# Weights' tiles moved to another offset in their buffers: 64 and 128 bytes between what TensorE moves and what it loads next

## The chip, the cores and the metric

The kernel runs on 1 core of a Trainium2 chip. The metric is the device time of one execution in microseconds (us). Before the change the median of 3 runs is 1715.13 us (1715.05 to 1716.48).

## The reference

One layer of an encoder block runs on two groups of tokens, 256 (prompt) and 512 (sample), with the same weights, all in float32. D_MODEL is 1024. What matters here are the first dense products of the layer:

```
h    = rmsnorm(x, norm_mix_g)
proj = h @ w_in                       # 1024 x 8192
u, q, k, v, qm, gl = split(proj)      # S5 input, differential attention's q, k, v,
                                      # memory attention's queries, gate logits
kv   = rmsnorm(mem, mem_norm_g) @ w_mem_kv   # keys and values of 256 memory tokens a group
```

u goes through a state-space model (S5), q, k, v through attention with two softmax maps a head, qm with kv through cross-attention. The three results are projected (w_branch), gated with sigmoid(gl + b_gate), summed and projected (w_out); then comes a gated feed-forward network (w_gate_up, w_down). Results are added to x.

## The kernel before

**Products in three parts.** A float32 operand is split into a high part (rounded to float32r) and a low part (the rest). `mm3` (L845 to L848) makes one product of two split operands from three matmuls: high x high (L846), high x low (L847) and low x high (L848). In a matmul, TensorE holds one operand still (the stationary one, 128 x 128, which a weight load, LDWEIGHTS, brings in ahead) and streams the other (the moved one, here mostly 256 columns). While one matmul streams, the next one's stationary operand is loaded.

**Which operand is which.** `dense_fm` (L850) gives feature-major results: the weights are stationary, the activations move. It makes gl (L1263, 12 pairs of weights' tiles, 256 columns a matmul), the memory queries mq (L1021) and u (L1225, 256 and 512 columns). `dense_tm` (L870) gives token-major results: the activations are stationary, the weights move. It makes qk (L1329), v (L1361), and the memory keys mk (L980) and values mv (L1001), all with 256 moved columns. The activations are H (the normed x, made by `whole_pair`, L938) and MT (the normed memory, called memThi and memTlo). A sum over 1024 features takes 8 steps of `mm3`, so 24 matmuls make one output tile; this document calls them a unit.

**The weights' stream.** `WStream` (L541) holds an ordered list of weights' pieces (`W.add`, L780 to L815), each with a kind. `_dma` (L572) loads half a piece with a DMA on SP's queue; `_split` (L667) splits it into a tile wh and a tile wl: ACT copies the high part (L679), and the low part is either subtracted by VectorE (L685) or, while `by_dma` is set (from gl on, L1256), copied negated by ACT (L682) and completed by a DMA on POOL's queue that adds (L683). `get` (L697) hands out the piece that is next and has the piece after it split. `_tile` (L586) allocates a pair of tiles in the pools whi and wlo, 4 buffers each. A tile has 1024 + 64 columns, of which 1024 are used; the used ones begin at column 0, or at column 32 where `shift` is set, which is the case for pieces of kind "s": the queries of memory and the gate logits. The tiles are 1088 x 4 = 4352 bytes apart, a multiple of 256. The very first piece (the first head's keys of memory) is not split by `_split` but piecemeal in the preamble (L1133 to L1142).

H's tiles are 6144 + 64 and 6144 + 16 columns, of which the first 16 are skipped (`c0=16`, L938). The order of the products is: keys, values and queries of memory, mixed with the attention over memory (to about 285 us); u; gl with the state-space model's products between (285 to 583 us); qk and v with the attention's products between (585 to 855 us); then the branches and the feed-forward network, whose products have 384 or 512 moved columns apart from the first block's.

```
c0, room = (32 if shift else 0), (0 if extra else 64)
t = [p.tile([128, self.HALF + room], F32R, name=f"w{w}{i}", tag=f"w{w}")
     for p, w in zip(self.extra if extra else (self.ph, self.pl), "hl")]
return tuple(x[:, c0 : c0 + self.HALF] for x in t)
```

Of the kernel before, what the change touches and what calls it, by code (L numbers as in the profile page):

```python
# [540 lines left out]
class WStream:  # L541
# [42 lines left out]
        self.n_dma += 1  # L584

    def _tile(self, i, extra=False, shift=False):  # L586
        c0, room = (32 if shift else 0), (0 if extra else 64)
        t = [p.tile([128, self.HALF + room], F32R, name=f"w{w}{i}", tag=f"w{w}")
             for p, w in zip(self.extra if extra else (self.ph, self.pl), "hl")]
        return tuple(x[:, c0 : c0 + self.HALF] for x in t)  # L590
# [120 lines left out]
def hybrid_block(ctx, tc, A, outs, consts):  # L711
# [17 lines left out]
    W = WStream(nc, tc, ctx)  # L729
# [38 lines left out]
    def cols(name, c0, n=256):  # L768
        w = A[name]
        return w.rearrange("(k p) c -> p k c", p=128)[:, :, c0 : c0 + n]  # L770
# [8 lines left out]
                 ("v", 3), ("q", 3)]  # L779
    for what, h in MEM_ORDER:  # L780
        c0 = {"k": 0, "v": 1024, "q": 4096}[what] + 256 * h
        W.add(cols("w_in" if what == "q" else "w_mem_kv", c0), 8, 256, "s" if what == "q" else None)
    for c in range(4):
        W.add(cols("w_u", 256 * c), 8, 256)
    for c in range(12):
        W.add(cols("w_in", 5120 + 256 * c), 8, 256, "s")
    for h in DIFF_HEADS:
        if h is None:
            W.add(cols("w_in", 3072 + 256 * vp), 8, 256)
        else:  # L790
            W.add([cols("w_in", 1024 + 128 * h, 128), cols("w_in", 2048 + 128 * h, 128)], 8, 256)
            vp = h // 2
    for nme in ("w_branch2", "s5_w_glu", "w_branch0", "w_branch1"):
        for c in range(4):
# [309 lines left out]
    with tc.tile_pool(name="nrm", bufs=1) as pool, tc.tile_pool(name="nrmg", bufs=1) as pg:  # L1104
# [19 lines left out]
        for k in range(8):  # L1124
            q, n = nc.sync if k else nc.scalar, 1 if k < 4 else 2
# [4 lines left out]
                pin(nc.scalar.dma_start(cg, A["gcols"]))  # L1130
        W.n_dma = W.n_split = 2
        W._dma()
        wp = [W._tile(f"0_{h}") for h in range(2)]  # L1133
        W.parts[0] = wp
        pss = [psd("mk"), env.psa("mk"), psd("mk"), env.psa("mk")]
        for k in range(8):
# [1085 lines left out]
```

## Time and profile before

| | |
|---|---|
| median of 3 runs | 1715.13 us |
| the profiled execution | 1715.91 us |
| its span, first to last instruction | 1714.1 us |
| granted TensorE clock, mean | 1.000 |
| TensorE (PE), matmuls | 1700.2 us busy, 99% of the span, 12082 matmuls |
| TensorE's weight loads (PEld) | 1624.3 us, 95% |
| VectorE (DVE) | 1313.2 us, 77% |
| ScalarE (ACT) | 931.8 us, 54% |
| GpSimd (POOL) | 337.1 us, 20% |

In the profile, a group's row has the source line, the engine, the operation, the tiles written and read, the shape, the count, then the busy time in us, the mean duration in ns, and the idle time before. A row of the timeline has the start in us, the duration in us, and the instruction. Matmuls are pipelined: a new one starts while the one before is still shown as running, and the ends are modelled. So the time that a matmul takes from the stream is the step from its start to the next one's start; durations serve to compare matmuls of one shape.

### The profile page before, as it was taken

The page shows a single profiled execution, that of the slowest core. Times are in us where ns is not written, and L with a number is a line of the kernel's source. Part 1 is how long each engine was busy: PE and PEld are TensorE (multiplying, and loading weights), DVE is VectorE, ACT ScalarE, POOL GpSimd, SP SyncE. Part 2 cuts the span into 40 slices and gives each one's busy share as a digit, 9 for nine tenths or more (in the row PEclk, how much of TensorE's full clock was granted, in tenths as well). Part 3 has the DMA queues.
Part 4 walks back from the last instruction along what each step waited for, and adds up shares of the span by engine and source line. Part 5 has one row for each costly group of instructions (what it writes and reads, how often), then busy time and mean ns, then how long its engine had stood idle before and what let it go on. Part 6 is the DMA issues. An engine that isn't in the chain of part 4 may idle for free.

```text
span 1714.1 us, 31468 instructions
## 1 busy us (share of the span) xinstructions
PE 1700.2 (99%) x12082; PEld 1624.3 (95%) x12082; DVE 1313.2 (77%) x2383; ACT 931.8 (54%) x1957; POOL 337.1 (20%) x403
## 2 busy tenths in 40 slices
PE   9999999999999999999999999999999999999999
PEld 9999988999999999999989999998889898989897
DVE  6876556999997459889876687792698868687876
ACT  6554536766665357778766564552444545454541
POOL 0040510000000111001210111430114334343420
PEclk9999999999999999999999999999999999999999
DMA  8433456676656446565964445672314448484733
GB/s 298 166 97 102 136 170 151 153 187 176 170 152 165 129 108 144 132 154 135 209 134 131 162 148 171 153 214 72 87 49 115 137 113 192 114 192 115 173 119 108
DMA packets 206758, 250.02 MB, mean 146 GB/s; under 512 B 34272, under 2 KB 162800, under 8 KB 206608
## 3 DMA queue, kind: packets, MB, share of 16 engines
q1 hardware_dynamic: 162896, 155.70, 30.0%
q0 software_dynamic: 32480, 67.01, 20.5%
q10 hardware_dynamic: 11232, 25.31, 4.3%
q8 instruction: 95, 1.56, 0.4%
q14 instruction: 55, 0.45, 0.1%
HBM read 173.51 MB, written 52.17 MB: 132 GB/s over the span
## 4 chain that ended last, share of the span: by engine, by line
PE 81%; issue 10%; DMA 4%; DVE 3%; ACT 1%; POOL 0%; SPq 0%; POOLq 0%; ACTq 0%; DVEq 0%
PE br L846 4%; PE br L847 4%; PE br L848 4%; PE up L846 3%; PE up L847 3%; PE up L848 3%; PE gate L847 3%; PE gate L848 3%; PE gate L846 3%; PE dn L846 3%; PE dn L848 3%; PE dn L847 3%; PE qk L847 3%; PE qk L846 3%; PE qk L848 3%
## 5 line engine op out<-in xcount | busy, mean ns | idle before, releaser
L846 PE MATMUL gl<-Hhi,wh 128*128 128x256 f32 x576 | 164.7, 286 | 0.5 <-ACT glt L1264 0.3
L847 PE MATMUL gl<-Hlo,wh 128*128 128x256 f32 x576 | 160.4, 278 | 0.0
L848 PE MATMUL gl<-Hhi,wl 128*128 128x256 f32 x576 | 160.2, 278 | 0.0
L679 ACT ACTIVATE wh<-wr 128x1024 fp32r<-128x1024 f32 x116 | 122.3, 1056 | 51.7 <-PE u L847 10.8
L683 POOL DMA_DIRECT2D wl<-wr x46 | 40.2, 874 | 463.5 <-ACT wl L682 440.3
L685 DVE TENSOR_TENSOR wl<-wr,wh 128x1024 fp32r<-128x1024 f32 x70 | 85.8, 1227 | 38.7 <-ACT wh L679 37.1
L846 PEld LDWEIGHTS gl<-Hhi,wh 128*128 128x128 f32 x576 | 108.4, 188 | 3.4 <-issue 1.8
L848 PEld LDWEIGHTS gl<-Hhi,wl 128*128 128x128 f32 x576 | 108.8, 189 | 0.0
L847 PEld LDWEIGHTS gl<-Hlo,wh 128*128 128x128 f32 x576 | 108.4, 188 | 0.2 <-issue 0.2
L846 PE MATMUL qk<-wh,Hhi 128*128 128x256 f32 x384 | 107.6, 280 | 0.0
L847 PE MATMUL qk<-wl,Hhi 128*128 128x256 f32 x384 | 107.5, 280 | 0.0
L848 PE MATMUL qk<-wh,Hlo 128*128 128x256 f32 x384 | 107.2, 279 | 0.0
L602 ACT ACTIVATE wh_S<-ws 128x512 fp32r<-128x512 f32 x91 | 53.9, 625 | 67.0 <-PE up L847 27.8
L607 DVE TENSOR_TENSOR wl_S<-ws,wh_S 128x512 fp32r<-128x512 f32 x91 | 67.0, 757 | 28.9 <-ACT wh_S L602 28.8
L846 PEld LDWEIGHTS qk<-wh,Hhi 128*128 128x128 f32 x384 | 72.3, 188 | 0.8
L848 PEld LDWEIGHTS qk<-wh,Hlo 128*128 128x128 f32 x384 | 72.3, 188 | 0.5
L847 PEld LDWEIGHTS qk<-wl,Hhi 128*128 128x128 f32 x384 | 72.2, 188 | 0.5
L1436 ACT ACTIVATE p<-sc,nm 128x512 f32<-128x512 f32 (+1 forms) x96 | 59.0, 617 | 13.2 <-DVE nm L1434 12.8
L1434 DVE TENSOR_REDUCE nm<-sc 128x1 f32<-128x512 f32 (+1 forms) x96 | 56.7, 599 | 11.5 <-PE sc L1428 10.5
L628 POOL TENSOR_TENSOR ws<-wr,ws 128x512 f32<-128x512 f32 x26 | 38.8, 1492 | 126.1 <-DVE wl_S L607 106.8
L602 ACT ACTIVATE wh_A<-wr 128x512 fp32r<-128x512 f32 x65 | 38.1, 623 | 39.0 <-PE up L847 17.3
L1264 ACT ACTIVATE glt<-gl,bg 128x256 f32<-128x256 f32 x72 | 33.6, 466 | 46.4 <-PE gl L848 34.8
(704 smaller groups left out, 6324.9 us busy)
## 6 DMA issues: line engine op xcount, KB each, us to landing
wl<-wr POOLq DMA_DIRECT2D x46, 512.0 KB, 5.6
wr<-in_w_gate_up_dram SPq DMA_DIRECT2D x44, 512.0 KB, 4.1
wr<-in_w_in_dram SPq DMA_DIRECT2D x40, 512.0 KB, 4.8
wr<-in_w_branch_dram SPq DMA_DIRECT2D x24, 512.0 KB, 3.9
wr<-in_w_down_dram SPq DMA_DIRECT2D x22, 512.0 KB, 4.4
gl_scr<-glt SPq DMA_DIRECT2D x72, 128.0 KB, 3.6
wr<-in_w_in_dram SPq DMA_DIRECT2D x32, 256.0 KB, 4.4
wr<-in_w_mem_kv_dram SPq DMA_DIRECT2D x14, 512.0 KB, 5.1
```

What stands on the lines that cost most here:

```text
L602: self.nc.scalar.activation(f(hi), src, AF.Copy)
L607: self.nc.vector.tensor_tensor(out=f(lo), in0=src, in1=f(hi).bitcast(F32), op=ALU.subtract)
L628: gt(out=s4, in0=A12, in1=s2, op=sub)
L679: self.nc.scalar.activation(hi, r, AF.Copy)
L683: self.nc.gpsimd.dma_start(lo, r.bitcast(F32R), accum_op=ALU.add)
L685: self.sub.tensor_tensor(out=lo, in0=r, in1=hi.bitcast(F32), op=ALU.subtract)
L846: pe.matmul(ps, wh, xh, start=start, stop=False)
L847: pe.matmul(ps, wh, xl, start=False, stop=False)
L848: pe.matmul(ps, wl, xh, start=False, stop=stop)
L1264: act.activation(gt[:, 0:n], ps[:, 0:n], AF.Identity, bias=bg[:, M : M + 1])
L1434: v.tensor_reduce(out=nm[:, m : m + 1], in_=ps, axis=AX.X, op=ALU.max, negate=True)
L1436: act.activation(pm[:, 0:n], ps, AF.Exp, bias=nm[:, m : m + 1], accum_out=s1s[:, tt : tt + 1] if m == 0 else s2)
```

## The change

The used columns of a tile of kind "s" begin at column 48 in place of 32. The keys and values of memory and the products of q with k and of v become kind "s" too, and the preamble's first pair of tiles is shifted in the same way. u, the branches and the feed-forward network are not touched. Sizes, the number of instructions and their order in the source stay.

```
     def _tile(self, i, extra=False, shift=False):
-        c0, room = (32 if shift else 0), (0 if extra else 64)
+        c0, room = (48 if shift else 0), (0 if extra else 64)
...
-        W.add(cols("w_in" if what == "q" else "w_mem_kv", c0), 8, 256, "s" if what == "q" else None)
+        W.add(cols("w_in" if what == "q" else "w_mem_kv", c0), 8, 256, "s")
...
     for h in DIFF_HEADS:
         if h is None:
-            W.add(cols("w_in", 3072 + 256 * vp), 8, 256)
+            W.add(cols("w_in", 3072 + 256 * vp), 8, 256, "s")
         else:
-            W.add([cols("w_in", 1024 + 128 * h, 128), cols("w_in", 2048 + 128 * h, 128)], 8, 256)
+            W.add([cols("w_in", 1024 + 128 * h, 128), cols("w_in", 2048 + 128 * h, 128)], 8, 256, "s")
...
-        wp = [W._tile(f"0_{h}") for h in range(2)]
+        wp = [W._tile(f"0_{h}", shift=True) for h in range(2)]
```

## The prediction

> **What bounds the kernel now.** I read the page first, then the groups by line with shapes kept apart, then the timeline of TensorE alone in narrow windows, because only starts are measured there: ends of matmuls are modelled.
>
> ```profile
> span 1714.1 us, 31468 instructions
> ...
> PE 1700.2 (99%) x12082; PEld 1624.3 (95%) x12082; DVE 1313.2 (77%) x2383; ACT 931.8 (54%) x1957; POOL 337.1 (20%) x403
> ...
> PE 81%; issue 10%; DMA 4%; DVE 3%; ACT 1%; POOL 0%; SPq 0%; POOLq 0%; ACTq 0%; DVEq 0%
> ```
>
> TensorE is busy 99% of the span and is 81% of the chain that ended last. So a nanosecond more or less between two matmuls moves the end by a nanosecond, wherever it stands. The profiled execution took 1715.91 us, 1.8 us more than its span, and 0.78 us more than the median of 1715.13.
>
> These are the matmuls that the change touches, all with 256 moved columns:
>
> ```profile
> L846 PE MATMUL gl<-Hhi,wh 128*128 128x256 f32 x576 | 164.7, 286 | 0.5 <-ACT glt L1264 0.3
> L847 PE MATMUL gl<-Hlo,wh 128*128 128x256 f32 x576 | 160.4, 278 | 0.0
> L848 PE MATMUL gl<-Hhi,wl 128*128 128x256 f32 x576 | 160.2, 278 | 0.0
> L846 PE MATMUL qk<-wh,Hhi 128*128 128x256 f32 x384 | 107.6, 280 | 0.0
> ...
> L847 PE MATMUL v<-wl,Hhi 128*128 128x256 f32 x192 | 54.0, 281 | 0.0
> ...
> L847 PE MATMUL mq<-Hlo,wh 128*128 128x256 f32 x192 | 54.0, 282 | 0.6 <-DVE Hlo L839 0.6
> ...
> L846 PE MATMUL mv<-wh,memThi 128*128 128x256 f32 x128 | 36.5, 285 | 0.8 <-DVE Vl L842 0.8
> ...
> L846 PE MATMUL mk<-wh,memThi 128*128 128x256 f32 x128 | 35.8, 282 | 0.3
> ```
>
> Each group has three lines (L846 to L848), so there are 3 x (576 + 384 + 192 + 192 + 128 + 128) = 4800 of them.
>
> They run at two rates, though shapes, source lines and clock are the same:
>
> ```profile
> 587.70 0.28 PE L846 MATMUL qk<-wh,Hhi 128*128 128x256 f32 x1
> ...
> 612.18 0.28 PE L846 MATMUL v<-wh,Hhi 128*128 128x256 f32 x1
> ...
> 296.72 0.28 PE L848 MATMUL gl<-Hhi,wl 128*128 128x256 f32 x1
> ...
> 298.84 0.28 PE L848 MATMUL gl<-Hhi,wl 128*128 128x256 f32 x1
> ```
>
> From 587.70 to 612.18 lie nine units of 24 matmuls (five of qk, four of v): 24.48 us / 216 = **113.3 ns** each. From 296.72 to 298.84 lie 18: **117.8 ns**. I call them the fast and the slow rate. Each lasts until something interrupts the stream. The durations tell them apart, so shares can be read off the groups:
>
> ```profile
> L848 PE MATMUL gl<-Hhi,wl x9: 276/276/278, 306.9 to 309.6; 128*128 128x256 f32 x9
> ...
> L848 PE MATMUL gl<-Hhi,wl x8: 281/281/281, 296.4 to 298.8; 128*128 128x256 f32 x8
> ```
>
> A fast stretch shows 276 ns and a slow one 281 (min/median/max). The gl lines L847 and L848 have a mean of 278: (278 - 276) / 5 = 0.4, so about **40% run slowly**. The other groups' means (280 to 285) are mixed with restarts after other products, so I take the 0.4 for all.
>
> **The change part by part.** It adds and removes no instruction. It moves where in a tile of 1088 columns the 1024 used ones begin. In the program's allocation, modulo 256 bytes, a weights' tile begins at 160; H, with its 16 columns skipped, and memT at 224. The distance that I count is from the moved operand to the next stationary one, which TensorE loads beside it.
>
> - gl and mq: the weights are loaded and H is moved. 32 columns (128 bytes) become 48 (192): the tile goes from 32 to 96, the distance from 64 to **128**.
> - qk, v, mk, mv and the preamble's first mk: the weights are moved and H or memT is loaded. 0 becomes 48 columns: from 160 to 96, the distance from 64 to **128**.
> - u, and the products with 384 or 512 moved columns, stay as they are.
>
> So all 4800 matmuls are at 64 now and at 128 afterwards. No steady stream in this trace is at 128. What other distances show:
>
> ```profile
> 1226.16 0.28 PE L848 MATMUL up<-fhi,wl 128*128 128x256 f32 x1
> ...
> 1228.68 0.28 PE L848 MATMUL up<-fhi,wl 128*128 128x256 f32 x1
> ...
> 204.71 0.28 PE L846 MATMUL u<-Hhi,wh 128*128 128x256 f32 x1
> ...
> 207.32 0.28 PE L848 MATMUL u<-Hhi,wl 128*128 128x256 f32 x1
> ...
> 248.93 0.28 PE L846 MATMUL u<-Hhi,wh 128*128 128x256 f32 x1
> ...
> 251.41 0.28 PE L846 MATMUL u<-Hhi,wh 128*128 128x256 f32 x1
> ```
>
> The first FFN block with 256 columns is at 0: 2.52 us / 21 = **120 ns**. u is at 192: 2.61 / 23 = 113.5 ns in one unit and 2.48 / 21 = 118.1 in another. So 0 is bad, and its two neighbours 64 and 192 are alike, fast or slow by how the stream was entered. If it is a collision of two reads that recurs every 256 bytes, 128 is farthest from it. I take that value: at 128 the stream settles at the fast rate. This is the nearest I have to a reason, not a measurement.
>
> The sum: 40% of 4800 are 1920 matmuls, at 117.8 - 113.3 = 4.5 ns: **-8.6 us**. Some of it stays, since a stream needs a few matmuls to become fast after another product has stood between:
>
> ```profile
> 299.65 0.39 PE L846 MATMUL gl<-Hhi,wh 128*128 128x256 f32 x1
> 299.87 0.28 PE L847 MATMUL gl<-Hlo,wh 128*128 128x256 f32 x1
> 299.99 0.28 PE L848 MATMUL gl<-Hhi,wl 128*128 128x256 f32 x1
> 300.11 0.28 PE L846 MATMUL gl<-Hhi,wh 128*128 128x256 f32 x1
> ```
>
> The first step here takes 220 ns, the next two 120 each, against 113.3. That is some 14 ns a restart, beside the first step, which the change doesn't touch. The mean of gl's L846 is 8 ns above its neighbours', and a first matmul is shown with 390 in place of 280: 576 x 8 / 110 = 42 restarts in gl, some 115 in 4800 matmuls, 1.6 us. Net: -8.6 + 1.6 = **-7 us**.
>
> Costed at nothing: ACT, DVE and the adding DMA write weights at another offset of the same size. That transfer shows no price for the offset, in the stretch of gl (tile at 32) and then in that of qk and v (at 160), and it lands while TensorE works on the weights before:
>
> ```profile
> wl<-wr POOLq DMA_DIRECT2D x20, 512.0 KB, 5.6
> ...
> wl<-wr POOLq DMA_DIRECT2D x20, 512.0 KB, 5.4
> ```
>
> One pair of weights' tiles of gl feeds 2 x 3 x 24 = 144 matmuls, some 16 us, which cover a transfer. Without that cover the 0.2 us between the two rows would be 8 us on 40 transfers. A TensorE faster by 7 us in some 850 us is not late for anything: idle time in front of the eight groups above is 2.2 us in all.
>
> The Trainium skill, "TensorE: Matmul & The Clock Gate", section "Step-by-step: what each phase is for", speaks against the change: "Loading the next tile's weights doesn't steal SBUF read bandwidth from the running matmul." By it the offset is immaterial and the sum is 0. The rows at 120 and 113.3 ns, with one shape, lean against it, but no row here has the same product at two offsets.
>
> **The rivals.**
>
> *The slow rate takes over (slower).* The mechanism: at 128 the load of the next weights collides with the moved stream in the phase in which it now runs free. Single steps at 128 are in the trace, where one product gives way to another:
>
> ```profile
> 130.21 0.28 PE L848 MATMUL ms<-kTh,mql 128*128 128x256 f32 x1
> 130.33 0.28 PE L846 MATMUL mv<-wh,memThi 128*128 128x256 f32 x1
> ...
> 140.04 0.28 PE L848 MATMUL ms<-kTh,mql 128*128 128x256 f32 x1
> 140.16 0.28 PE L848 MATMUL mv<-wh,memTlo 128*128 128x256 f32 x1
> 140.28 0.28 PE L846 MATMUL mq<-Hhi,wh 128*128 128x256 f32 x1
> ...
> 124.72 0.28 PE L848 MATMUL mq<-Hhi,wl 128*128 128x256 f32 x1
> 124.84 0.28 PE L846 MATMUL mv<-wh,memThi 128*128 128x256 f32 x1
> 124.96 0.28 PE L847 MATMUL mv<-wl,memThi 128*128 128x256 f32 x1
> ```
>
> Both steps from ms to mv are at 128, and so is the one from mv to mq at 140.16; mq to mv at 124.72 is at 0. By these rows each takes 0.12 us; the unrounded starts make it 118 ns for the two into mv, after a stream at 113, and 114 for the one at 0. For the rival: 128 costs 4 to 5 ns at once, 0 does not. Against it: after the step at 0 the next one (124.84 to 124.96) is late instead, and the step after a 128 is short (140.16 to 140.28 is 115 unrounded). Any jump of addresses seems to cost some 5 ns in two steps, whatever the distance. Price: today's mean is 113.3 + 0.4 x 4.5 = 115.1; at 117.8 for all, 4800 x 2.7 = +13 us, **1728**; with seven of ten slow, 4800 x 0.3 x 4.5 = +6.5, 1722. It decides as soon as over 40% + 0.2% of 1715 / (4800 x 4.5 ns) = 56% run slowly. Its far end is a collision that recurs every 128 bytes: then 128 is like 0 and 4800 x (120 - 115.1) = +23.5 us, 1739. That 64 and 192 are alike fits it too.
>
> *The change does nothing.* Both rates stay with their shares, since how a stream is entered decides and not the distance: **1715**, within 3 us. For it: 64 and 192 show the same two rates. Against it: at 0 there is one rate, and another. The rule of the Trainium skill quoted above, from "TensorE: Matmul & The Clock Gate", would give this time too.
>
> *More than the fast rate.* Weights alone set this floor:
>
> ```profile
> 414.23 1.50 PE L431 MATMUL psI<-U,ET 128*128 128x99 f32 x12
> 415.57 0.39 PE L468 MATMUL psY<-U,TT 128*128 128x97 f32 x2
> ```
>
> Twelve matmuls with 99 columns take 1.34 us, 111.7 ns each, though they move fewer columns. At that rate 4800 x (115.1 - 111.7) = -16 us, **1699**.
>
> **How the numbers follow.** Fast rate for all or nearly all: 0.41, 1705 to 1711. The floor of the loads: 0.03. Nothing: 0.14, 1712 to 1718. The slow rate more often than now: 0.34, 1719 to 1728, and like 0, 1739: 0.08. The likeliest single case is the first: 1715.1 - 7 = **1708**; its own range is 1705 to 1711. Cases of both signs hold much, so the range goes from 1705, below which lie the floor and a little of the first case, to 1726, above which lie the end of the slow case and the 1739: some 0.17 left out. Faster by over 0.2% (3.4 us, about what a measurement of this kernel can tell from no change) 0.44, within 0.14, slower 0.42.
>
> **What would show it.** Right: the durations of gl, qk, v, mq, mv and mk have medians of 276 and their L847 and L848 means within 1 ns of it in gl; steps of 113.3 ns in long stretches, none of 117.8 for a whole unit; u and all with 384 and 512 columns as before. Wrong, by the rival: medians of 281 and steps of 117.8, or of 120 throughout. Wrong altogether: the same stretches slow as now (gl at 296) and the mean 278 again, or a change of time in stages after 860 us, where no tile has moved.

## The result and the profile after

| | before | after |
|---|---|---|
| median | 1715.13 us (5 runs, 1714.31 to 1717.49) | 1726.72 us (5 runs, 1725.01 to 1727.77) |
| ratio | | 1.0062, 95% interval 1.005 to 1.0074 |
| span of the profiled run | 1714.1 us | 1724.9 us |

The change makes the kernel slower by 11.6 us in the medians and by 10.8 us in the profiled spans; the ratio stands for 10.6 us. The forecast was 1708 us, so its sign is wrong; the time lies 0.7 us above the top of the range.

First the head of the page of after (span, busy time by engine, shares of the chain that ended last), to be held against the same three lines of before:

```profile
span 1724.9 us, 31468 instructions
...
PE 1713.7 (99%) x12082; PEld 1639.2 (95%) x12082; DVE 1314.7 (76%) x2383; ACT 932.1 (54%) x1957; POOL 335.2 (19%) x403
...
PE 43%; DVE 2%; issue 1%; DMA 0%; ACT 0%; ACTq 0%; DVEq 0%; POOLq 0%
```

TensorE is busy 13.5 us longer with the same 12082 matmuls, while the span grows by 10.8 us: TensorE's idle time has shrunk by 2.7 us. The order of the instructions is the same on every engine, and VectorE, ScalarE and GpSimd change by 2 us at most. (The chain's shares can't be held against those of before: in after the chain is followed back only to 923 us, where it begins with a DMA, in before nearly to the start.)

The groups of after, by line with shapes kept apart (count, then busy us and mean ns of one, then idle time before):

```profile
L846 PE MATMUL gl<-Hhi,wh 128*128 128x256 f32 x576 | 167.0, 290 | 0.0
L847 PE MATMUL gl<-Hlo,wh 128*128 128x256 f32 x576 | 162.6, 282 | 0.0
L848 PE MATMUL gl<-Hhi,wl 128*128 128x256 f32 x576 | 162.6, 282 | 0.0
L846 PE MATMUL qk<-wh,Hhi 128*128 128x256 f32 x384 | 108.9, 284 | 0.0
...
L847 PE MATMUL v<-wl,Hhi 128*128 128x256 f32 x192 | 54.5, 284 | 0.0
...
L847 PE MATMUL mq<-Hlo,wh 128*128 128x256 f32 x192 | 54.4, 284 | 0.0
```

All three lines of gl rise by 4 ns, qk by 4, v by 3, mq by 2, though shape, order and clock (1.000) are as before. Durations are modelled ends, so the proof is in the starts. The timeline of TensorE alone in after, first and last row of two stretches: the nine units of qk and v that the prediction timed, and 24 matmuls of gl.

```profile
308.73 0.29 PE L848 MATMUL gl<-Hhi,wl 128*128 128x256 f32 x1
...
311.61 0.28 PE L848 MATMUL gl<-Hhi,wl 128*128 128x256 f32 x1
...
592.73 0.28 PE L846 MATMUL qk<-wh,Hhi 128*128 128x256 f32 x1
...
618.37 0.28 PE L846 MATMUL v<-wh,Hhi 128*128 128x256 f32 x1
```

qk and v: 25.64 us / 216 = **118.7 ns**, where before took 113.3. gl: 2.88 us / 24 = **120 ns**; the same 24 matmuls took 2.72 us / 24 = 113.3 ns in before (306.90 to 309.62). The fast rate is gone everywhere.

Where the time went, from all starts of both traces. In the products that the change touches (gl, qk, v, mq, mk, mv) the steps under 126 ns between two matmuls of one product, some 4465 of 4800, have a mean of 115.13 ns before and 118.71 after: 513.8 us become 530.7, +16.9. The longer steps of these products (first ones after another product, waits) shrink from 55.6 to 53.0 us, -2.6. All other products together take 3.5 us less. Sum: +10.8, which is the difference of the spans.

That some of the loss is absorbed shows in the waits of TensorE (who waited, for whom; us, times, longest). Before:

```profile
PE psK L356 <- ACT Ysb L472: 1.4, 2, 1.0
...
PE br L862 <- DMA Hhi<-mo_scrh: 1.3, 1, 1.3
...
PE mv L846 <- DVE Vl L842: 0.8, 2, 0.6
...
PE mq L847 <- DVE Hlo L839: 0.6, 1, 0.6
```

and after, where the wait of mq is gone and one of sc, a product of the attention, is new:

```profile
PE sc L1427 <- ACT p L1436: 1.1, 2, 0.7
...
PE psK L356 <- ACT Ysb L472: 0.5, 1, 0.5
PE mv L846 <- DVE Vl L842: 0.4, 1, 0.4
...
PE br L862 <- DMA Hhi<-mo_scrh: 0.2, 1, 0.2
```

A slower TensorE arrives later at operands that were not ready in time before. By the end of v the lag is 10.7 us. Behind it the shorter wait of br takes it down to 9.5, and around the waits of sc it comes back to 10.8. Two matmuls of later stages in after, and the same two (by their place in TensorE's order) in before:

```profile
1010.89 0.33 PE L846 MATMUL br<-XT1h,wh_S 128*128 128x384 f32 x1
...
1721.25 0.28 PE L848 MATMUL dn<-wh,lA2l 128*128 128x256 f32 x1
```

```profile
1000.03 0.33 PE L846 MATMUL br<-XT1h,wh_S 128*128 128x384 f32 x1
...
1710.45 0.28 PE L848 MATMUL dn<-wh,lA2l 128*128 128x256 f32 x1
```

The lag is 10.86 us at the first and 10.80 at the last: where no tile has moved, it stays.

### The profile page after: what moved, and what is told of

Read it like the earlier page. It is cut to its first block, busy times and chain, and to the rows that moved or that the text cites. A ratio compares the mean times of both kernels' runs of the same rounds, so it can differ in the third digit from the quotient of the medians.

```text
span 1724.9 us, 31468 instructions
## 1 busy us (share of the span) xinstructions
PE 1713.7 (99%) x12082; PEld 1639.2 (95%) x12082; DVE 1314.7 (76%) x2383; ACT 932.1 (54%) x1957; POOL 335.2 (19%) x403
## 5 line engine op out<-in xcount | busy, mean ns | idle before, releaser
L846 PE MATMUL gl<-Hhi,wh 128*128 128x256 f32 x576 | 167.0, 290 | 0.0
L847 PE MATMUL gl<-Hlo,wh 128*128 128x256 f32 x576 | 162.6, 282 | 0.0
L848 PE MATMUL gl<-Hhi,wl 128*128 128x256 f32 x576 | 162.6, 282 | 0.0
L846 PEld LDWEIGHTS gl<-Hhi,wh 128*128 128x128 f32 x576 | 108.9, 189 | 2.5 <-issue 1.8
L847 PEld LDWEIGHTS gl<-Hlo,wh 128*128 128x128 f32 x576 | 108.9, 189 | 0.2 <-issue 0.2
L846 PE MATMUL qk<-wh,Hhi 128*128 128x256 f32 x384 | 108.9, 284 | 0.0
L847 PE MATMUL qk<-wl,Hhi 128*128 128x256 f32 x384 | 108.9, 284 | 0.0
L848 PEld LDWEIGHTS gl<-Hhi,wl 128*128 128x128 f32 x576 | 108.8, 189 | 0.0
L848 PE MATMUL qk<-wh,Hlo 128*128 128x256 f32 x384 | 108.5, 283 | 0.0
L846 PEld LDWEIGHTS qk<-wh,Hhi 128*128 128x128 f32 x384 | 72.3, 188 | 0.9
L847 PEld LDWEIGHTS qk<-wl,Hhi 128*128 128x128 f32 x384 | 72.3, 188 | 0.6
L848 PEld LDWEIGHTS qk<-wh,Hlo 128*128 128x128 f32 x384 | 72.3, 188 | 0.5
L1436 ACT ACTIVATE p<-sc,nm 128x512 f32<-128x512 f32 (+1 forms) x96 | 58.8, 615 | 11.6 <-DVE nm L1434 11.2
```

The lines of the kernel that those rows point to most:

```text
L846: pe.matmul(ps, wh, xh, start=start, stop=False)
L847: pe.matmul(ps, wh, xl, start=False, stop=False)
L848: pe.matmul(ps, wl, xh, start=False, stop=stop)
L1436: act.activation(pm[:, 0:n], ps, AF.Exp, bias=nm[:, m : m + 1], accum_out=s1s[:, tt : tt + 1] if m == 0 else s2)
```

## The experiments

**Theory:** what counts is the distance, modulo 256 bytes, from the operand that a matmul moves to the one that TensorE loads beside it, and 64 is a good distance where 128 is not. **Rivals:** it is the place of the weights' tile itself (96 in the changed kernel) or of where they are written; 128 is bad because every distance but a few is, or because it is far from 64; the cause is a matmul's own pair of operands and not the load beside it. In most of the kernels below, `_tile` takes the column at which the used part begins from the piece's kind:

```
-    def _tile(self, i, extra=False, shift=False):
-        c0, room = (32 if shift else 0), (0 if extra else 64)
+    def _tile(self, i, extra=False, shift=0):
+        c0, room = shift, (0 if extra else 64)
...
-        hi, lo = self._tile(f"{i}_{h}", kind == "x" and h == 0, kind == "s")
+        hi, lo = self._tile(f"{i}_{h}", kind == "x" and h == 0, kind if isinstance(kind, int) else 0)
```

With H where it was, column c gives gl and mq the distance 4c - 64, and qk, v, mk and mv 64 - 4c. Where a mean step is given, it is over all steps under 126 ns between two matmuls of one product.

### All products at 192, 0, 32 and 96

d192 (the others differ only in the columns):

```
-        W.add(cols("w_in" if what == "q" else "w_mem_kv", c0), 8, 256, "s" if what == "q" else None)
+        W.add(cols("w_in" if what == "q" else "w_mem_kv", c0), 8, 256, 0 if what == "q" else 32)
...
-        W.add(cols("w_in", 5120 + 256 * c), 8, 256, "s")
+        W.add(cols("w_in", 5120 + 256 * c), 8, 256, 0)
...
-            W.add(cols("w_in", 3072 + 256 * vp), 8, 256)
+            W.add(cols("w_in", 3072 + 256 * vp), 8, 256, 32)
...
-            W.add([cols("w_in", 1024 + 128 * h, 128), cols("w_in", 2048 + 128 * h, 128)], 8, 256)
+            W.add([cols("w_in", 1024 + 128 * h, 128), cols("w_in", 2048 + 128 * h, 128)], 8, 256, 32)
...
-        wp = [W._tile(f"0_{h}") for h in range(2)]
+        wp = [W._tile(f"0_{h}", shift=32) for h in range(2)]
```

In d0 all columns are 16; in d32 gl and mq have 24 and the others 8; in d96 gl and mq have 40 and the others 56.

> All 4800 matmuls at a distance of 192 bytes (gl and mq: column 0; qk, v, mk, mv: column 32). Theory A, the cost recurs every 128 bytes: 192 is like 64, two rates of 113 and 118 ns, a time of 1715 +- 3 us. Theory B, it recurs only every 256 bytes and 128 is simply a bad place of it: 192 need not be like 64; by u's units, most of them slow, 1720 to 1728. Theory C, not the distance but the place of the weights' tile (96 in the changed kernel) is bad: the tiles lie at 160 and at 32 here as they do before the change, so 1715.

> All at a distance of 0 (column 16 for all: tiles at 224). Theory A: 0 is like 128, mean step 118.7 ns or the 120 of the first FFN block, a time of 1725 to 1735 us. Theory B: 0 is worse than 128, 120 ns throughout, 1733 to 1738. Theory C: the tile is at 224, a new place; nothing follows.

> All at a distance of 32 (gl and mq: column 24; qk, v, mk, mv: column 8). Theory A: half way between bad 0 and good 64; equal to 160, and if the cost falls steadily 1718 to 1724 us. Theory B: between 0 and 64 too, 1720 to 1728. Neither expects under 1715 unless 64 is not the best place.

> All at a distance of 96 (gl and mq: column 40; qk, v, mk, mv: column 56). Theory A: between good 64 and bad 128, by symmetry about 64 the time of the run at 32. Theory B: nothing links it to 32; if the cost rises steadily from 64 to 128, 1718 to 1724 us. A time under 1712 would mean that 64 was not the best place.

Measured, beside before (1714.87 us in 8 runs taken together with these kernels) and after (whose ratio goes by its own before, 1715.13 us):

| kernel | distance | mean step gl, qk, ns | median us | ratio and interval |
|---|---|---|---|---|
| before | 64 | 115.2, 114.8 | 1714.87 | |
| d192 | 192 | 116.8, 117.6 | 1721.20 | 1.0036 (1.0023 to 1.005) |
| d96 | 96 | 118.2, 118.3 | 1724.53 | 1.0059 (1.0044 to 1.0074) |
| d32 | 32 | 118.3, 118.2 | 1724.56 | 1.0060 (1.0043 to 1.0077) |
| after | 128 | 119.0, 118.5 | 1726.72 | 1.0062 (1.005 to 1.0074) |
| d0 | 0 | 119.6 to 119.9 | 1728.15 | 1.0081 (1.0066 to 1.0096) |

The nine units of qk and v in the timelines of d192, then d0, then d96:

```profile
589.50 0.28 PE L846 MATMUL qk<-wh,Hhi 128*128 128x256 f32 x1
...
614.94 0.28 PE L846 MATMUL v<-wh,Hhi 128*128 128x256 f32 x1
```

```profile
593.61 0.28 PE L846 MATMUL qk<-wh,Hhi 128*128 128x256 f32 x1
...
619.53 0.28 PE L846 MATMUL v<-wh,Hhi 128*128 128x256 f32 x1
```

```profile
590.78 0.28 PE L846 MATMUL qk<-wh,Hhi 128*128 128x256 f32 x1
...
616.42 0.28 PE L846 MATMUL v<-wh,Hhi 128*128 128x256 f32 x1
```

25.44, 25.92 and 25.64 us for 216 matmuls: 117.8, 120.0 and 118.7 ns. Theory A is out with 192, which isn't like 64, and so is theory C, which had 1715 us there. Of theory B, 192 (1721 us) and the 120 ns at 0 (119.7) came true, its 1733 us at 0 did not: the median of d0 is 13.3 us above that of before. 32 and 96 take the same time, just above the 1718 to 1724 us of a steady slope. So 64 is the best of six distances, 192 comes second (it keeps fast stretches, some 20% of the steps in gl and 5% in qk), and 128 is no special case: it is where 32 and 96 are. Nor does time fall with the way from 0. The rule that the prediction weighed, from the Trainium skill, "TensorE: Matmul & The Clock Gate", section "Step-by-step: what each phase is for" (loading the next weights takes nothing from the running matmul's reads), does not hold here: one product, in one order, takes 113.3 or 120.0 ns by the offset alone.

### The distance kept, the places moved

In h_moved, H begins 64 bytes lower and the weights follow: gl and mq at column 16, qk and v at 48, so that all distances stay 64. The tiles of qk and v then lie at 96, exactly where the changed kernel has them. (Only u and other users of H get other distances: u goes from 192 to 0, where its matmuls with 256 columns take 119.6 ns, as expected.)

```
-    def whole_pair(nm, c0=16):
+    def whole_pair(nm, c0=0):
...
+        W.add(cols("w_in", 5120 + 256 * c), 8, 256, 16)
...
+            W.add(cols("w_in", 3072 + 256 * vp), 8, 256, 48)
```

> H's used columns begin at 0 in place of 16 (at 160 modulo 256), and the weights' tiles follow: gl and mq at 224 (column 16), qk and v at 96 (column 48, as in the changed kernel); mk and mv as before the change. So the distance is 64 in all six, with the places moved. Theory D (the distance alone counts): gl, mq, qk and v keep means of 115 to 115.5 ns and some 55% to 70% fast steps, 1715 +- 3 us; u goes to a distance of 0, its 256-column matmuls to 120 ns. Rival P (the place of the weights' tile or of H counts): qk and v, at 96 as in the changed kernel, stay at 118 to 119 ns, and the time is 1718 us or more.

Measured: 1714.50 us, ratio 0.9999 (0.999 to 1.0009). The same nine units:

```profile
587.65 0.28 PE L846 MATMUL qk<-wh,Hhi 128*128 128x256 f32 x1
...
612.13 0.28 PE L846 MATMUL v<-wh,Hhi 128*128 128x256 f32 x1
```

24.48 us / 216 = 113.3 ns, with the weights at the changed kernel's place. The place is out; the distance is what the change spoiled. That only the distance modulo 256 counts shows within this stretch and its twin in before: steps of the sum and tiles change both addresses by multiples of 256 bytes (1024 for the weights, 3072 for H, 4352 from tile to tile), and every one of the 216 steps in before is 113 or 114 ns.

Moving the weights also moves, by as much, where ACT, VectorE and the adding DMA write the next tiles, so those writes could be what gets in the way. The trace of after answers that for gl: 225 steps during which ACT or VectorE splits weights have a mean of 119.1 ns, the other 1403 have 119.0; 499 steps within 5.5 us of the issue of an adding DMA have 118.9, the others 119.0. The steps are long whether something is written or not.

The other way round, aligned puts H and the weights at multiples of 64 bytes, with a distance for each product: gl and qk 64, v 192, mq 128, in columns 24, 56, 24 and 40, H at column 8.

```
-    def whole_pair(nm, c0=16):
+    def whole_pair(nm, c0=8):
```

> H's used columns begin at column 8 (192 modulo 256) in place of 16, so that H and the weights of gl, mq, qk and v lie at multiples of 64 bytes; so far they lay 32 bytes past one, in every kernel. Distances: gl and qk 64, v 192, mq 128; mk and mv untouched at 64. Theory D (the distance alone): gl and qk 114.5 to 115.5 ns, v 117, mq 118.6, the times of the same distances before. Rival L (the place against a line of 64 bytes counts too): other means at the same distances, lower if the extra line that a tile beside the line takes is what costs. u moves to a distance of 224, where single steps with 512 columns took over 231 ns against 229: some +1 us that belongs to neither.

Measured: 1717.62 us, ratio 1.0009 (1.0 to 1.0019). gl 114.9, qk 114.8, v 116.9, mq 118.8 ns, each within 0.3 ns of what the same distance gave it in before, d192 or after. In its groups, gl and qk have the durations of before and only mq is longer:

```profile
L847 PE MATMUL gl<-Hlo,wh 128*128 128x256 f32 x576 | 160.1, 278 | 0.0
L847 PE MATMUL qk<-wl,Hhi 128*128 128x256 f32 x384 | 107.5, 280 | 0.0
L847 PE MATMUL mq<-Hlo,wh 128*128 128x256 f32 x192 | 54.6, 285 | 0.3 <-DVE Hlo L839 0.3
```

Being aligned adds nothing of its own. u, at 224 here, takes 233.2 ns a step with 512 columns against 229.5 at 192 in before, some 0.7 us in all, of the +1 that was expected.

### How wide the good place is

Two kernels with a distance for each product. scan1: gl 56, mq 60, qk 72, v 80, mk and mv 48. scan2: gl 72, mq 68, qk 56, v 48, mk and mv 160.

```
+        W.add(cols("w_in" if what == "q" else "w_mem_kv", c0), 8, 256, 31 if what == "q" else 4)
...
+        W.add(cols("w_in", 5120 + 256 * c), 8, 256, 30)
...
+            W.add(cols("w_in", 3072 + 256 * vp), 8, 256, 60)
...
+            W.add([cols("w_in", 1024 + 128 * h, 128), cols("w_in", 2048 + 128 * h, 128)], 8, 256, 62)
```

> Five distances in one kernel, one a product: mk and mv 48, gl 56, mq 60, qk 72, v 80 (before the change: all 64). Means of the steps, 64 having 115.1, 32 having 118.3 and 96 having 118.1 ns. Theory N (64 is a narrow good place): within 16 bytes of 64 the mean is already 117 ns or more. Theory W (a wide one, falling evenly): 48 and 80 at 116.7, 56 and 72 at 115.9, 60 at 115.5. A better place than 64 would show a mean under 115.

> The same with the roles exchanged: gl 72, mq 68, qk 56, v 48, and mk and mv at 160. Theory D: gl at 72 as qk at 72 in the scan before it, qk at 56 as gl at 56 there, v at 48 as mk there, within 0.5 ns, though moved and loaded operand are exchanged. 160 lies half way between 128 (118.7) and 192 (117.0): 117.8 ns, or 118.2 if every 128 bytes repeat (as 32).

Measured: 1728.01 and 1727.3 us, one run each. In scan1 and then scan2 the groups of gl (278 before):

```profile
L847 PE MATMUL gl<-Hlo,wh 128*128 128x256 f32 x576 | 161.7, 281 | 0.0
```

```profile
L847 PE MATMUL gl<-Hlo,wh 128*128 128x256 f32 x576 | 162.1, 281 | 0.0
```

Mean steps: 117.9 at 56, 118.4 at 60, 118.4 at 68, 118.3 at 72 for the products that load the weights. Four bytes beside 64 the gain is gone: the good place is narrow, and a good place that fades slowly with the distance is ruled out. qk, which moves the weights, has 120.2 at 56 and 119.9 at 72, where gl has 117.9 and 118.3. So at these distances the distance alone does not tell the rate: it also matters which operand is the moved one, or where the moved one begins, which these two kernels don't tell apart. Nor is 160 like 32 (118.3), as was thought possible, or half way between 128 and 192: mk and mv take 120.0 ns there, as at 0. At 48 (mk and mv in scan1, v in scan2) it is 118.5 to 118.9, at 80 (v) 119.2.

### One part of the change at a time

gl_only is the kernel before with gl alone at 128; all_but_gl is the changed kernel with gl back at 64.

```
-        W.add(cols("w_in", 5120 + 256 * c), 8, 256, "s")
+        W.add(cols("w_in", 5120 + 256 * c), 8, 256, 48)
```

> Only gl is at 128, all else as before the change. Theory D: gl's mean goes from 115.2 to 118.9 ns, 1628 steps x 3.7 ns = 6 us, the other groups keep theirs: 1721 +- 2 us, and the rest of the change's 11.6 us (some 5.5) belongs to qk, v, mq, mk. Rival P gives the same. A rival that the loss comes from the shifted tiles of qk, v and the memory's products alone: 1715.

> The changed kernel with gl back at 64 (column 32). With gl_only it makes up the whole change, whose ratio is 1.0062. If the parts add up, its ratio is 1.0062 - 0.0023 = 1.004, 1722 us; by the steps (3.7 ns on 1059 of qk, 3.1 on 525 of v, 3.4 on 526 of mq, 4.3 on 369 of mk, 2.5 on 360 of mv) +9.8 us, 1725. If a fast gl lets an entry elsewhere go over to the fast rate or the slow one, it lies outside both.

Measured: gl_only 1718.78 us, ratio 1.0023 (1.0013 to 1.0033); all_but_gl 1721.86 us, 1.0040 (1.0025 to 1.0055). 0.0023 + 0.0040 = 0.0063, against 0.0062 for the whole change: the parts add up by the ratios; by the steps, 1725 us was expected for all_but_gl. gl, qk and v change only where they were moved (mq, mk and mv, shorter products, differ by up to 0.7 ns where they were not). gl_only's timeline, gl and then qk and v:

```profile
305.38 0.29 PE L848 MATMUL gl<-Hhi,wl 128*128 128x256 f32 x1
...
308.26 0.28 PE L848 MATMUL gl<-Hhi,wl 128*128 128x256 f32 x1
...
589.34 0.28 PE L846 MATMUL qk<-wh,Hhi 128*128 128x256 f32 x1
...
613.82 0.28 PE L846 MATMUL v<-wh,Hhi 128*128 128x256 f32 x1
```

gl 120 ns (2.88 / 24) and qk, v 113.3 (24.48 / 216). All of gl's steps add up to 6.2 us more, yet the median is 4.1 us above the 1714.7 of before beside it (1721 +- 2 us was expected), and the profiled span only 1.6 us above. Part of the gap is named by the group of psK, the state-space model's product that stands between units of gl. In gl_only, then in all_but_gl:

```profile
L356 PE MATMUL psK<-G,par 64*32 64x128 f32 x512 | 13.0, 275 | 0.5 <-ACT Ysb L472 0.5
```

```profile
L356 PE MATMUL psK<-G,par 64*32 64x128 f32 x512 | 13.5, 275 | 1.4 <-ACT Ysb L472 1.4
```

Its steps sum to 1.7 us less than before in gl_only and the same as before in all_but_gl. Another 1.5 us of the profiled run are mv's, which nothing moved; why it was faster is not shown. Over all runs psK is cheaper by 0.5 to 2.2 us whenever gl is off 64, and never when gl is at 64: a slower gl covers a wait for ACT, 0.9 us of it by the two rows.

### Which operands are compared

low_apart: in gl and mq only the low tile (wl) moves to 96; wh stays at 32. Then L847 moves Hlo while wl is loaded, at 128; L846 and L848 load wh, at 64. If instead a matmul's own stationary tile counted, L848 (which uses wl) would be the slow one.

```
-        return tuple(x[:, c0 : c0 + self.HALF] for x in t)
+        return t[0][:, c0 : c0 + self.HALF], t[1][:, c0 + 16 * (c0 == 32) : c0 + 16 * (c0 == 32) + self.HALF]
```

> The kernel before the change, but in gl and mq only the low parts' tiles are moved, from 32 to 96. So one load in three, the one of wl, which runs beside the matmul of L847, is at 128 and the other two at 64. Theory N (the moved stream collides with the next weights' load): the step that follows L847's start is the long one, 117 ns or more on average, or no step stays at the fast rate because the stream never settles: gl's mean between 115.2 and 119. Rival O (a matmul collides with its own weights): L848, the only one whose own weights lie at 128, has the long step. Rival Q (the distance between stream and load isn't what counts, but that all three are alike): the mean is above 119.

Measured: 1719.08 us, ratio 1.0025 (1.0016 to 1.0035). gl's three lines:

```profile
L846 PE MATMUL gl<-Hhi,wh 128*128 128x256 f32 x576 | 167.0, 290 | 0.0
L847 PE MATMUL gl<-Hlo,wh 128*128 128x256 f32 x576 | 162.3, 282 | 0.0
L848 PE MATMUL gl<-Hhi,wl 128*128 128x256 f32 x576 | 161.0, 279 | 0.0
```

Steps by the matmul that starts them: L846 119.0, **L847 119.5**, L848 116.2 ns; in mq 118.9, 119.5 and 116.4. The line with 128 beside it is the longest and the one whose own tile moved is the shortest, so it is the load beside the matmul that counts. (The trace shows them side by side: in before and after each load of gl starts within 10 ns of the start of the matmul ahead of its own.) But one bad load in three costs gl nearly all (mean 118.3 against 119.0 with all three): L846 is slow at 64 too, and no stretch of three steps at 114 ns or less is left in gl or mq. Why L846 and not L848 carries it on is not shown.

### Products with 384 and 512 columns

wide is the kernel before with other columns for later products: w_branch2 48 (distance 128), s5_w_glu 32 (128), w_branch0 16 (0), w_out 32 (128) and 48 (64). The matmul lines are one higher there.

```
-            W.add(cols("w_out", 512 * c, 512)[:, 4 * kh : 4 * kh + 4], 4, 512)
+            W.add(cols("w_out", 512 * c, 512)[:, 4 * kh : 4 * kh + 4], 4, 512, 48 if c else 32)
```

> The kernel before the change, with other distances for products with more moved columns: the first half of s5_w_glu (384 columns) at 128, w_branch2's (256, 384 and 512) at 128 in place of 192, w_branch0's at 0, w_out's first half (512) at 128 and its second at 64 in place of 0. Theory S (a collision costs only where the weights' load has no time to spare: alone it needs 112 ns, a matmul with 384 columns takes 173 and one with 512 takes 227): 173.4 ns at every distance, 227 to 230 at every distance, 1715 +- 2 us. Rival M (the moved stream itself is held up): 384 and 512 columns lose the 4 to 6 ns at 128 too, which is some 3 us on the 288 matmuls of w_out, 192 of w_glu and 350 of w_branch2.

Measured: 1718.35 us, ratio 1.0018 (1.0008 to 1.0028). 192 matmuls of wo with 512 columns, in before and then in wide:

```profile
1154.30 0.39 PE L846 MATMUL wo<-wh,mgd_1556hi 128*128 128x512 f32 x1
...
1197.82 0.39 PE L846 MATMUL wo<-wh,mgd_1556hi 128*128 128x512 f32 x1
```

```profile
1153.46 0.40 PE L847 MATMUL wo<-wh,mgd_1556hi 128*128 128x512 f32 x1
...
1198.25 0.39 PE L847 MATMUL wo<-wh,mgd_1556hi 128*128 128x512 f32 x1
```

43.52 / 192 = 226.7 ns at 0, 44.79 / 192 = 233.3 ns, at 128 in the first half of w_out and at 64 in the second alike. With 384 columns 128 takes 176.0 ns (glu) against 173.4 at 0. The median is 2.9 us above the 1715.49 of before beside it, the some 3 us of rival M. Twelve matmuls with 99 columns, each with its load, took 111.7 ns each (psI, in the prediction), so beside 512 columns a load has room to be late. If only the load were held up, these products should not have changed; that the moved stream itself is held up is what is left, though no trace shows the two reads. And for 512 columns the best of the distances seen is 0, one of the worst for 256.

## Why the prediction was wrong

- **What bounds the kernel: right in the main.** The lag of 10.7 us at the end of v is, at 10.8, there at the last matmul. But the prediction let every nanosecond between two matmuls move the end by one, wherever it stands; of 16.9 us, 10.8 came through, as a slower stream covers waits.
- **Which matmuls change: right.** The 4800 with 256 columns; gl_only and all_but_gl show that gl, qk and v each answer to their own distance.
- **Two rates, 40% slow: right.** From the starts, gl's mean of 115.19 is (115.19 - 113.3) / 4.5 = 42% slow, the whole 115.13.
- **The step that failed:** "If it is a collision of two reads that recurs every 256 bytes, 128 is farthest from it. I take that value: at 128 the stream settles at the fast rate." Six distances show no such shape: 64 has 115.1 ns, 192 about 117, and 0, 32, 96 and 128 all 118 to 120; h_moved, with the tiles of qk and v where the change put them but the distance at 64, is at 113.3. 64 is not half way to something better but a narrow good place. The term of -8.6 us came out as +16.9 us.
- **"0 is bad, and its two neighbours 64 and 192 are alike"** failed with it: u's few units showed both rates at both distances, but not the shares. With all products at 192 the slow rate prevails.
- **The evidence that was set aside.** The two steps at 128 that end at 130.33 and 140.16 us took 117 and 118 ns (the prediction has 118 for both), longer than the fast rate as the steady stream at 128 is (118.7). They were discounted because a step at 0 took 114. That step misled: a steady stream at 0 takes 120. But that the two came so close to 118.7 is partly luck: the third step at 128, from 140.16 us, took 115, and in after the nine units of qk and v go through steps of some 119, 115, 118, 122 and 120 ns again and again, while the 24 matmuls of gl shown above take 120. A single step could not tell the mean.
- **The rival "the slow rate takes over": right**, in mechanism and nearly in size. It took 117.8 ns for all, +13 us and 1728; measured are 118.71 ns and +16.9 us, of which 6 us are absorbed by waits and other products, which the rival left out, and 1726.72 came out. Two errors that offset each other brought it so close. Its far end (128 like 0, 1739) would have needed 120 ns throughout and no absorption; even d0, with 119.7, took only 1728.15.
- **"The change does nothing": wrong**, as 1.0062 shows.
- **The restarts' +1.6 us** were not told apart: the first steps got shorter with the slower stream, -2.6 us with the waits among them.
- **Nothing for ACT, DVE and the DMA: right.** In after the same splits take the same time, by line and by the DMA's issues between 300 and 580 us (median from issue to landing last):

```profile
L685 DVE TENSOR_TENSOR wl<-wr,wh 128x1024 fp32r<-128x1024 f32 x70 | 85.7, 1225 | 39.8 <-ACT wh L679 39.0 <-PE mq L848 0.6
L682 ACT ACTIVATE wl<-wr 128x1024 fp32r<-128x1024 f32 x46 | 48.3, 1050 | 2.7 <-PE v L847 1.6 <-PE qk L847 1.1
```

```profile
wl<-wr POOLq DMA_DIRECT2D x22, 512.0 KB, 5.5
```

The same three had 1227 ns, 1051 ns and 5.6 us in before.

What stays open: why 64 and, half as good, 192 are good distances, and what in the memory lies behind it. The runs show which addresses go well together, and that the load beside the matmul is one of the two; no run looks into the memory. Nor does any of these kernels beat the kernel before: h_moved equals it.

## What to carry to other kernels

Where TensorE is the bound and runs short matmuls back to back, the offset of a tile is a parameter of the kernel: measure it by the step from start to start in long undisturbed stretches, one product at a time, and do not argue from a symmetry which offset is good. Single steps at the new offset, if the trace has some, can hint at the direction, but they miss the steady rate: at 128 they took 115 to 118 ns where the stream's mean is 118.7, at 0 one took 114 where the stream takes 120. And count what a slower bound absorbs: 16.9 us of longer steps became 10.8 us of span.

## What was not expected of the hardware

- Four bytes matter: with 256 moved columns a matmul's step is 115.1 ns on average at a distance of 64 bytes, and 118.4 at 60 and at 68.
- The good distance depends on the width of the moved operand: for 512 columns 0 is best (226.7 ns) of those seen and 64 costs 233.3; for 256 columns 0 (120.0) is among the worst.
- At 64 the share of the fast rate varies by itself. In h_moved nothing about mk and mv was changed, and their means went from 114.3 and 116.2 to 116.4 and 116.7 ns. The prediction put the shares down to how a stream is entered; no run shows what sets them, and a nanosecond or two on these short products proves nothing.
- A distance need not have one rate: at 128 some stretches take 120 ns a step (gl), others repeat five steps of 115 to 122 ns with a mean of 118.7 (qk and v).
- One bad load in three is enough to keep a stream off the fast rate (118.3 ns in low_apart).
